# A hybrid encoder layer on one core: residual tiles of the down projection loaded further ahead into four buffers, and the hidden frames loaded by ScalarE's queue

## The chip, the cores and the metric

The kernel runs on one NeuronCore of a Trainium2 chip. TensorE multiplies; VectorE, ScalarE and GpSimd compute beside it; SyncE, ScalarE and GpSimd can each call DMA transfers, which all run on the core's 16 DMA engines. The metric is the device time of one execution in microseconds; lower is better. Each engine works through its own instructions in order and waits for the others by semaphores, so an instruction that waits holds up everything behind it on its engine.

## The reference

One layer of a streaming encoder over 576 frames (512 of a prompt, 64 of a sample), in float32. Attention and short convolution come first; the part that the change touches is the end, the feed-forward network with its residual:

```python
x = x + mix @ w_out
h2 = rmsnorm(x, g_norm2)
x = x + (jax.nn.silu(h2 @ w_gate) * (h2 @ w_up)) @ w_down
```

The model width is 2048, the hidden width D_FF 5632. The outputs are x and the new rows of the key, value and convolution caches.

## The kernel before

Everything is kept transposed: channels on the 128 partitions, the 576 frames as columns in two halves of 288. Every float32 operand is split into a high and a low part, and each product is made of three matmuls (high x high, low x high, high x low). The split of a weight takes ScalarE a cast and VectorE a subtraction; its result is the tile `whl` (L217, L218).

Gate, up and down projection run in *units*. A unit multiplies 256 output channels by 2m input blocks of 128 with a seven-product scheme in Strassen's manner: the weights are read as four quarters a11, a12, a21, a22, the frames come in seven prepared forms, and the products are numbered 1 to 7. Units 0 to 41 (NGU = 42) are gate and up, in turn; 42 to 77 are the 36 down units that the list `DOWN` names as (output pair d, first hidden pair, last hidden pair). There are 8 output pairs and 22 hidden pairs, so each output pair is worked on in several units; unit 42 takes (0, 0, 3), unit 47 (0, 3, 7), unit 53 (3, 4, 8), unit 70 is the first that finishes an output pair. Below, (41,4) is product 4 of unit 41. The products of neighbouring units are interleaved: (n+1,1), (n,3), (n,4), (n+1,2), (n+1,6), (n+1,7), (n+1,5). Their weights are prepared two products ahead in program order (`AHEAD`).

Four kinds of transfer run in the down units:

- **Weights**: two loads `raw` a unit on SyncE's queue (L180), rows of 512 B. There are two buffers for each, so a load waits until the unit two before it has used its own. VectorE's sum `s` (L1052) needs the second.
- **Frames**: the seven forms of a hidden pair. The up units write them, form by form (`form`, L923, GpSimd), to `hid_dram`. `load_pair` (L1141, GpSimd) reads one pair back into one of seven slots: 2016 KB, one row of 16,128 B for each partition. Three slots lie where the second norm's result was, four where its sums were; later pairs reuse a slot when all output pairs are past it. `calls` says after which unit.
- **Residual tiles**: `load_x2` (L1126, GpSimd) reads two blocks of 128 x 576 of x (576 KB) when the unit begins, into one of two buffers; the unit's seven products are added there (L1135, VectorE); after product 4 `store_x2` (L1130, GpSimd) writes it back for the next unit of the same output pair. A unit that finishes a pair turns its tile on TensorE and writes the output instead (`store_y`).
- **Outputs**, from unit 70 on, GpSimd and ScalarE.

Only TensorE's order is written out by hand. That of the other engines, SyncE's and GpSimd's DMA calls among them, is laid out by a scheduler from its own estimates when the kernel is built: an instruction that can go earlier by them stands earlier in its engine's order, whatever its place in the program.

Of the kernel before, what the change touches and what calls it, by code (L numbers as in the profile page):

```python
# [10 lines left out]
F32 = mybir.dt.float32  # L11
# [5 lines left out]
P = 128  # L17
TP = 512
TS = 64
T = TP + TS  # L20
HALF = T // 2
HALVES = ((0, HALF), (HALF, T))
# [15 lines left out]
SLOTS = 7  # L38
# [55 lines left out]
def tile_hybrid_stream_step(  # L94
# [6 lines left out]
    nc = tc.nc  # L101
# [14 lines left out]
    tmp = ctx.enter_context(tc.tile_pool(name="tmp", bufs=2, side="left"))  # L116
    acon = tc.alloc_tile_pool(name="acon", bufs=1, side="left")
    xt_dram = tc.dram_tile([KD, P, T], F32, name="xt_dram")
    x2_dram = tc.dram_tile([KD, P, T], F32, name="x2_dram")
    hid_dram = tc.dram_tile([NFP, P, FORMS, 2, HALF], F32, name="hid_dram")  # L120
# [23 lines left out]
    UNITS = [(kind, fp, 0, NP) for fp in range(1, NFP) for kind in ("gate", "up")]  # L144
    NGU = len(UNITS)
# [31 lines left out]
    def load_weight(i=None):  # L177
        i = len(raws) if i is None else i
        raws[i], raw3, src = weight_raw(i)
        nc.sync.dma_start(out=raw3, in_=src)  # L180
# [73 lines left out]
    def misc(name):  # L254
        return ps_z.tile([P, 512], F32, tag="misc", name=name, bufs=2)
# [104 lines left out]
    with tc.manual_schedule(engines={mybir.EngineType.Activation, mybir.EngineType.DVE, mybir.EngineType.SP}):  # L360
# [26 lines left out]
        for kt in range(KD + LAG):  # L387
# [19 lines left out]
            if kt in (14, 16):  # L407
                a = (kt - 14) * 512
# [53 lines left out]
    for i in range(5):  # L462
        n = P if i < 4 else TS
# [369 lines left out]
    h2pool = tc.alloc_tile_pool(name="h2pool", bufs=1, reuse_waits="tile", side="left")  # L833
# [168 lines left out]
    slots = {}  # L1002
# [13 lines left out]
    NU = len(UNITS)  # L1016
# [25 lines left out]
    def prepare(n, p_):  # L1042

        st = unit.setdefault(n, {})
        m = UNITS[n][3]
        if p_ == 1:
            st["a11"], st["a12"] = column(first_block + 2 * n, m)
        src = {1: "a11", 2: "a12", 3: "a12", 4: "a22", 5: "s1", 6: "a11", 7: "a21"}[p_]
        if p_ == 6:
            st["a21"], st["a22"] = column(first_block + 2 * n + 1, m)  # L1050
            st["s1"] = w2pool.tile([P, NP, P], F32, tag="s1", name="s1")[:, :m]
            nc.vector.tensor_tensor(out=st["s1"], in0=st["a21"], in1=st["a22"], op=ALU.add)  # L1052
            nc.vector.tensor_tensor(out=st["a21"], in0=st["a21"], in1=st["a11"], op=ALU.subtract)
            nc.vector.tensor_tensor(out=st["a11"], in0=st["s1"], in1=st["a11"], op=ALU.subtract)
        if p_ == 3:
            nc.vector.tensor_tensor(out=st["a12"], in0=st["a12"], in1=st["a11"], op=ALU.subtract)
        slot_turn[0] += 1
        whl = wpool.tile([P, 2, NP, P], F32R, tag=("whi", "wlo")[slot_turn[0] % 2], name="whl")[:, :, :m]
        split(whl[:, 0], whl[:, 1], st[src])
        operand[n, p_] = whl  # L1060
# [9 lines left out]
    def run(n, p_):  # L1070
        st = unit[n]
        kind, fp = UNITS[n][:2]

        def kept(tag):
            t = tmp.tile([P, HALF], F32, tag=tag, name="part", bufs=1)
            nc.scalar.copy(out=t, in_=st["y"])  # L1076
            return t

        def done(c, i, ps, part=None):
            if kind != "down":  # L1080
                return finish(kind, fp, c, i, ps, part)
            add(n, c, i, ps)
            if part is not None:
                add(n, c, i, part)
            if n in last:
                store_y(n, c, i)
            elif (c, i) == (1, 0):
                store_x2(n)

        if p_ == 1:  # L1090
            st["y"] = ps_pj.tile([P, HALF], F32, tag="pj", name="psy")
            multiply(st["y"], n, 1, True)
            st["p1"] = kept("ms")
        elif p_ == 2:
            x = ps_z.tile([P, 512], F32, tag="z0", name="psx2")[:, :HALF]
            multiply(x, n, 2, True)
            done(0, 0, x, st["p1"])
        elif p_ == 6:
            multiply(st["y"], n, 6, False)
            st["u2"] = kept("ms" if n == NGU - 1 else "t")  # L1100
        elif p_ == 7:
            st["w"] = ps_z.tile([P, 512], F32, tag=f"z{n % 2 + 1}", name="psw")[:, :HALF]
            multiply(st["w"], n, 7, True)
        elif p_ == 5:
            multiply(st["y"], n, 5, False)
            u4 = kept("acc")
            done(1, 1, st["w"], u4)
        elif p_ == 3:
            multiply(st["y"], n, 3, False)
            done(0, 1, st["y"])  # L1110
        else:
            multiply(st["w"], n, 4, False)
            done(1, 0, st["w"], st["u2"])
            del unit[n]


    last = {}
    for n in range(NGU, NU):
        last = {m_: 1 for m_ in last if UNITS[m_][1] != UNITS[n][1]} | {n: 1}
    xt2 = {}  # L1120
    down = {}

    def load_x2(n):
        d = UNITS[n][1]
        xt2[n] = down["pool"].tile([P, 2, T], F32, tag="x2", name=f"x2_{n}", bufs=2)
        nc.gpsimd.dma_start(out=xt2[n], in_=x2_dram[2 * d : 2 * d + 2].rearrange("k p t -> p k t"))  # L1126

    def store_x2(n):
        d = UNITS[n][1]
        nc.gpsimd.dma_start(out=x2_dram[2 * d : 2 * d + 2].rearrange("k p t -> p k t"), in_=xt2.pop(n))  # L1130

    def add(n, c, i, src):
        a, b = HALVES[i]
        dst = xt2[n][:, c, a:b]
        nc.vector.tensor_tensor(out=dst, in0=src, in1=dst, op=ALU.add)  # L1135

    def load_pair(p):
        tag = ("h2ah", "h2al", "b22", "s3", "s4", "s5", "s6")[p % SLOTS]
        pool = h2pool if p % SLOTS < 3 else down["pool"]
        slots[p] = pool.tile([P, FORMS, 2, HALF], F32R, tag=tag, name=f"slot{p}")  # L1140
        nc.gpsimd.dma_start(out=slots[p].bitcast(F32), in_=hid_dram[p])  # L1141

    def store_y(n, c, i):

        x2t, cs = xt2[n][:, c, :], slice((2 * UNITS[n][1] + c) * P, (2 * UNITS[n][1] + c + 1) * P)
        whole = (c, 1 - i) in unit[n].setdefault("done", set())
        unit[n]["done"].add((c, i))
        b0, b1 = ((0, 2), (3, 4), (0, 3), (2, 4))[2 * whole + i]

        def work():  # L1150
            yield 3
            ob = down["pool"].tile([P, 3, P], F32, tag="ob", name="ob", bufs=2)[:, : b1 - b0]
            po = misc("pot")[:, : (b1 - b0) * P]
            for q in range(b0, b1):
                nc.tensor.transpose(po[:, (q - b0) * P : (q - b0 + 1) * P], x2t[:, q * P : (q + 1) * P], ident)
            nc.vector.tensor_copy(out=ob, in_=po.rearrange("p (i c) -> p i c", c=P))
            nc.gpsimd.dma_start(out=yp[b0 * P : b1 * P, cs].rearrange("(i p) c -> p i c", p=P), in_=ob)
            if i:
                po2 = misc("pot2")
                nc.tensor.transpose(po2[:TS, :P], x2t[:, TP:], ident)  # L1160
                os_ = down["pool"].tile([TS, P], F32, tag="obs", name="obs", bufs=2)
                nc.scalar.copy(out=os_, in_=po2[:TS, :P])
                nc.scalar.dma_start(out=ys[:, cs], in_=os_)

        pipe.spawn(work())
# [4 lines left out]
    for k_, (n, p_) in enumerate(order):  # L1170
        if p_ == 1:
            for i in range(first_block + 2 * n, min(first_block + 2 * n + 4, len(specs))):
                if i not in raws:
                    load_weight(i)
        if (n, p_) == (NGU, 1):
            tpool.release()
            ypool.release()
            down["pool"] = tc.alloc_tile_pool(name="dpool", bufs=1, reuse_waits="tile", side="right")
            load_x2(n)
            load_pair(3)  # L1180
        if n > NGU and p_ == 1:
            load_x2(n)
            if n < NGU + SLOTS - 3:
                load_pair(n - NGU + 3)
        if k_ + AHEAD < len(order):
            prepare(*order[k_ + AHEAD])
        run(n, p_)
        if n == NGU - 1:
            for p in {2: (0, 1), 3: (2,)}.get(p_, ()):
                load_pair(p)  # L1190
        if n >= NGU and p_ == 4:
            for p in calls[n - NGU]:
                load_pair(p)
    pipe.flush()
# [34 lines left out]
```

## Time and profile before

| | before |
|---|---|
| median of 3 runs | 2506.39 us (2503.45 to 2511.66) |
| the profiled execution's own time | 2504.79 us |
| its span, first to last instruction | 2503.1 us |
| TensorE busy | 2425.3 us (97%), mean granted clock 0.989 |
| VectorE, ScalarE, GpSimd busy | 70%, 43%, 11% |
| DMA | 369.52 MB, mean 148 GB/s |
| first frame called, last frame called | 1905.1 us, 2333.3 us |
| frames, call to landing | 22 loads, 10.5 us median (8.8 to 20.4) |
| residual tiles, call to landing | 36 loads, 4.6 us median (4.0 to 16.6) |

In the profile's rows PE is TensorE, DVE VectorE, ACT ScalarE, POOL GpSimd, SPq SyncE's sequencer; L1066 is a line of the kernel. `psy<-slot,whl` is a matmul that writes the tile psy from the tiles slot and whl. What stands in brackets after a row of the timeline is the idle time of its engine just before it, and what ended it. A row of the waits reads: who waited, for whom, total us, times, longest. The windows give, for each stretch of the span, the busy time of every engine, the granted TensorE clock as a share, the busy share of the DMA engines and what they moved. DMA queue q0 is GpSimd's, q1 SyncE's.

### The profile page before, as it was taken

The numbers are of one execution on the slowest core, as the hardware profiler recorded it, in microseconds if no ns is written. First come the engines' busy times: TensorE is split into PE (matmuls) and PEld (weight loads), VectorE is DVE, ScalarE is ACT, GpSimd is POOL, SyncE is SP. The second block draws the span as 40 slices with busy tenths as digits, with TensorE's granted clock in tenths as the row PEclk, the third lists the DMA queues.
The fourth block names the chain that finished last, engine by engine and source line by source line (L and its number), as shares of the span: only waits on it lengthen the run. The fifth ranks groups of instructions, "written<-read, shape, count | busy, mean of one in ns | idle before, by whom it ended". The sixth has DMA issues, their size and how long they took to land.

```text
span 2503.1 us, 43901 instructions
## 1 busy us (share of the span) xinstructions
PE 2425.3 (97%) x18121; PEld 2412.5 (96%) x18121; DVE 1756.5 (70%) x2772; ACT 1070.0 (43%) x1863; POOL 282.8 (11%) x483
## 2 busy tenths in 40 slices
PE   8999999999999999999999999999998897999898
PEld 8999999999999999999999999999998897999798
DVE  7766666353345458888888888888886686877676
ACT  6655555231122345444444444444443343444333
POOL 2111011110020120000010000100001111101121
PEclk9999999999999999999999999999999998999899
DMA  8322332222242333445344454444545767868753
GB/s 266 86 87 86 90 90 83 68 85 85 85 161 85 103 136 107 135 144 158 120 144 140 148 155 126 140 137 149 154 133 209 278 195 265 262 220 288 257 155 92
DMA packets 441345, 369.52 MB, mean 148 GB/s; under 512 B 9854, under 2 KB 411896, under 8 KB 438328
## 3 DMA queue, kind: packets, MB, share of 16 engines
q1 hardware_dynamic: 413624, 233.39, 32.2%
q0 software_dynamic: 26240, 132.79, 14.4%
q8 instruction: 142, 2.33, 0.4%
q10 hardware_dynamic: 1280, 0.53, 0.1%
q14 instruction: 59, 0.48, 0.1%
HBM read 285.85 MB, written 80.82 MB: 146 GB/s over the span
## 4 chain that ended last, share of the span: by engine, by line
PE 88%; DMA 5%; issue 3%; DVE 2%; ACT 1%; POOL 0%; SPq 0%; POOLq 0%; DVEq 0%; ACTq 0%
PE psy L1066 29%; PE pj L209 23%; PE psw L1066 15%; PE pjo L209 8%; PE psx L1066 7%; DMA raw<-in_w_down_dram 4%; PE pw L981 2%; DVE whl L218 1%; PE z L547 1%; PE po L613 1%; DMA xin<-in_x_prompt_dram 0%; DVE x L1135 0%; DMA slot<-hid_dram 0%; PE os L643 0%; PE zs L573 0%
## 5 line engine op out<-in xcount | busy, mean ns | idle before, releaser
L217 ACT CAST whl<-raw 128x1024 fp32r<-128x1024 f32 (+5 forms) x468 | 419.0, 897 | 309.0 <-issue 106.4
L218 DVE TENSOR_TENSOR whl<-raw,whl 128x1024 fp32r<-128x1024 f32 (+5 forms) x468 | 481.4, 1029 | 89.1 <-ACT whl L217 87.7
L209 PE MATMUL pj<-xhi,whi 128*128 128x288 f32 x1504 | 450.0, 299 | 0.4 <-ACT whi L172 0.4
L209 PE MATMUL pj<-xlo,whi 128*128 128x288 f32 x1504 | 444.3, 295 | 1.7 <-DVE xlo L343 1.7
L209 PE MATMUL pj<-xhi,wlo 128*128 128x288 f32 x1504 | 443.9, 295 | 0.3 <-DVE wlo L173 0.3
L1066 PE MATMUL psy<-slot,whl 128*128 128x288 f32 x2112 | 304.8, 300 | 47.0 <-ACT part L1076 20.3
L1066 PEld LDWEIGHTS psy<-slot,whl 128*128 128x128 f32 x2112 | 291.2, 192 | 49.9 <-ACT part L1076 21.3
L209 PEld LDWEIGHTS pj<-xlo,whi 128*128 128x128 f32 x1504 | 283.6, 189 | 2.0 <-DVE xlo L343 2.0
L1066 PE MATMUL psw<-tsum,whl 128*128 128x288 f32 x2016 | 282.6, 296 | 2.8 <-DVE ut L960 2.8
L209 PEld LDWEIGHTS pj<-xhi,whi 128*128 128x128 f32 x1504 | 283.8, 189 | 1.0 <-ACT whi L172 0.6
L209 PEld LDWEIGHTS pj<-xhi,wlo 128*128 128x128 f32 x1504 | 283.9, 189 | 0.9 <-DVE wlo L173 0.5
L1066 PE MATMUL psy<-tsum,whl 128*128 128x288 f32 x2016 | 281.1, 295 | 1.2 <-DVE whl L218 1.2
L1066 PEld LDWEIGHTS psw<-tsum,whl 128*128 128x128 f32 x2016 | 273.4, 190 | 3.0 <-DVE ut L960 3.0
L1066 PEld LDWEIGHTS psy<-tsum,whl 128*128 128x128 f32 x2016 | 271.8, 189 | 1.5 <-DVE whl L218 1.5
L172 ACT CAST whi<-raw 128x1024 fp32r<-128x1024 f32 (+1 forms) x138 | 140.0, 1031 | 231.7 <-PE pj L209 95.8
L1076 ACT COPY part<-psy 128x288 f32<-128x288 f32 x234 | 93.4, 399 | 296.9 <-PE psy L1066 290.7
L923 POOL DMA_DIRECT2D hid_dram<-form x154 | 83.6, 543 | 914.0 <-DVE form L218 751.2
L173 DVE TENSOR_TENSOR wlo<-raw,whi 128x1024 fp32r<-128x1024 f32 (+1 forms) x132 | 160.3, 1227 | 23.9 <-ACT whi L172 22.6
L1066 PE MATMUL psw<-slot,whl 128*128 128x288 f32 x1056 | 155.5, 298 | 2.2 <-DVE x L1135 2.2
L1066 PEld LDWEIGHTS psw<-slot,whl 128*128 128x128 f32 x1056 | 146.0, 190 | 2.5 <-DVE x L1135 2.4
L1066 PE MATMUL psy<-b,whl 128*128 128x288 f32 x1008 | 140.4, 295 | 0.5 <-ACT part L1076 0.5
L1066 PE MATMUL psx<-h2ah,whl 128*128 128x288 f32 x672 | 135.6, 297 | 2.7 <-DVE gs L960 2.7
(336 smaller groups left out, 4208.1 us busy)
## 6 DMA issues: line engine op xcount, KB each, us to landing
raw<-in_w_in_dram SPq DMA_DIRECT2D x47, 1024.0 KB, 5.6
raw<-in_w_gate_dram SPq DMA_DIRECT2D x44, 1024.0 KB, 5.7
raw<-in_w_up_dram SPq DMA_DIRECT2D x44, 1024.0 KB, 6.3
hid_dram<-form POOLq DMA_DIRECT2D x154, 288.0 KB, 2.5
slot<-hid_dram POOLq DMA_DIRECT2D x22, 2016.0 KB, 10.5
x<-x_dram POOLq DMA_DIRECT2D x36, 576.0 KB, 4.6
raw<-in_w_down_dram SPq DMA_DIRECT2D x30, 640.0 KB, 5.8
raw<-in_w_out_dram SPq DMA_DIRECT2D x16, 1024.0 KB, 5.2
```

The source lines that it names most:

```text
L172: nc.scalar.copy(out=hi[:, a:b], in_=raw[:, a:b])
L173: lo_eng.tensor_tensor(out=lo[:, a:b], in0=raw[:, a:b], in1=hi[:, a:b].bitcast(F32), op=ALU.subtract)
L209: mm(ps, w_[:, k, csl], x_[:, k, a:b], start=(k == 0 and n == 0), stop=(k == nk - 1 and n == 2))
L217: nc.scalar.copy(out=hi, in_=src)
L218: (lo_eng or nc.vector).tensor_tensor(out=lo, in0=src, in1=hi.bitcast(F32), op=ALU.subtract)
L547: mm(zb[i], a_[:, kk], b_[:, q0:TP], start=(n == 0), stop=False, skip_group_check=True)
L613: mm(po[:, i * P : 512], a_[:, i, :], b_[:, : 512 - i * P], stop=(i == 0 and n == 2), **kw)
L923: nc.gpsimd.dma_start(out=hid_dram[fp][:, n - 1], in_=t.bitcast(F32))
L981: mm(pss[j, i], w_[:, k, j * P : (j + 1) * P], x_, start=(kk == 0 and k == 0 and n == 0), stop=(kk == 1 and k == 7 and n == 2))
L1066: mm(ps, whl[:, w_, j, :], x_, start=(start and j == 0 and q == 0), stop=(j == len(xs_) - 1 and q == 2), skip_group_check=True)
L1076: nc.scalar.copy(out=t, in_=st["y"])
```

## The change

A residual tile is called in earlier, and there are four places for it instead of two. Units whose number leaves 0 or 1 by four, and all from unit 70 on, use the two whole buffers as before. The other 14 (42, 43, 46, 47, ... 66, 67) use four pieces of 128 x 288 each, in temporary tiles that the gate and up units leave (tags y, r, sq, hx); these are loaded and stored by four DMAs each. The call for unit n+2 stands after product 4 of unit n in the program; before it stood at product 1 of the unit itself. And `load_pair` calls its transfer on ScalarE instead of GpSimd.

```diff
+    first_last = min(last)
+    spare = [(tmp, "y"), (tmp, "r")], [(tmp, "sq"), (h2pool, "hx")]
+
     def load_x2(n):
-        d = UNITS[n][1]
-        xt2[n] = down["pool"].tile([P, 2, T], F32, tag="x2", name=f"x2_{n}", bufs=2)
-        nc.gpsimd.dma_start(out=xt2[n], in_=x2_dram[2 * d : 2 * d + 2].rearrange("k p t -> p k t"))
+
+        d, xb = UNITS[n][1], {}
+        if n % 4 < 2 or n >= first_last:
+            whole = down["pool"].tile([P, 2, T], F32, tag="x2", name=f"x2_{n}", bufs=2)
+            nc.gpsimd.dma_start(out=whole, in_=x2_dram[2 * d : 2 * d + 2].rearrange("k p t -> p k t"))
+            xb["whole"] = whole
+        for c in range(2):
+            for i, (a, b) in enumerate(HALVES):
+                if "whole" in xb:
+                    xb[c, i] = whole[:, c, a:b]
+                    continue
+                pool, tag = spare[n % 2][c]
+                xb[c, i] = pool.tile([P, HALF], F32, tag=tag, name=f"x2_{n}", bufs=2)
+                nc.gpsimd.dma_start(out=xb[c, i], in_=x2_dram[2 * d + c][:, a:b])
+        xt2[n] = xb
 
     def store_x2(n):
-        d = UNITS[n][1]
-        nc.gpsimd.dma_start(out=x2_dram[2 * d : 2 * d + 2].rearrange("k p t -> p k t"), in_=xt2.pop(n))
+        d, xb = UNITS[n][1], xt2.pop(n)
+        if "whole" in xb:
+            nc.gpsimd.dma_start(out=x2_dram[2 * d : 2 * d + 2].rearrange("k p t -> p k t"), in_=xb["whole"])
+            return
+        for c, i in ((0, 0), (1, 1), (0, 1), (1, 0)):
+            a, b = HALVES[i]
+            nc.gpsimd.dma_start(out=x2_dram[2 * d + c][:, a:b], in_=xb[c, i])
 
     def add(n, c, i, src):
-        a, b = HALVES[i]
-        dst = xt2[n][:, c, a:b]
+        dst = xt2[n][c, i]
...
     def load_pair(p):
...
-        nc.gpsimd.dma_start(out=slots[p].bitcast(F32), in_=hid_dram[p])
+        nc.scalar.dma_start(out=slots[p].bitcast(F32), in_=hid_dram[p])
...
             load_x2(n)
             load_pair(3)
-        if n > NGU and p_ == 1:
-            load_x2(n)
-            if n < NGU + SLOTS - 3:
-                load_pair(n - NGU + 3)
+            load_x2(n + 1)
+        if NGU < n < NGU + SLOTS - 3 and p_ == 1:
+            load_pair(n - NGU + 3)
...
         if n >= NGU and p_ == 4:
+            if n + 2 < NU:
+                load_x2(n + 2)
             for p in calls[n - NGU]:
                 load_pair(p)
```

In the order that the scheduler gives the changed kernel, the call for a tile on GpSimd stands right after the store that frees its place, some two units earlier than before: that of unit 52 after the store of unit 48. The pieces of units 42 and 43 and the whole tiles of 44 and 45 stand among the last stores of `form`. On ScalarE the calls for slots 0 to 3 stand between the casts of the last forms, and the cast for (42,6) stands behind two of these casts, where it stood ahead of them before. On VectorE the weight part of (41,4) now stands ahead of the sum `s` of unit 42, where it stood behind it. TensorE's order is unchanged.

More of the change, by code (lines that the diff above doesn't have):

```diff
@@ L1140, in load_pair @@
         slots[p] = pool.tile([P, FORMS, 2, HALF], F32R, tag=tag, name=f"slot{p}")
-        nc.gpsimd.dma_start(out=slots[p].bitcast(F32), in_=hid_dram[p])
+        nc.scalar.dma_start(out=slots[p].bitcast(F32), in_=hid_dram[p])
     def store_y(n, c, i):
-        x2t, cs = xt2[n][:, c, :], slice((2 * UNITS[n][1] + c) * P, (2 * UNITS[n][1] + c + 1) * P)
+        x2t, cs = xt2[n]["whole"][:, c, :], slice((2 * UNITS[n][1] + c) * P, (2 * UNITS[n][1] + c + 1) * P)
         whole = (c, 1 - i) in unit[n].setdefault("done", set())
```

## Prediction

> **What bounds the kernel now.** TensorE carries the chain, so I read the last stage, the only one that the change touches, by windows, and then TensorE's waits in it.
>
> ```profile
> PE 88%; DMA 5%; issue 3%; DVE 2%; ACT 1%; POOL 0%; SPq 0%; POOLq 0%; DVEq 0%; ACTq 0%
> ```
> ```profile
> core 0: us, PE busy (x) PEld busy (x) DVE busy (x) ACT busy (x) POOL busy (x), PEclk, DMA share, GB/s
> 1905.00:1990.00 85.00, 64.36 (x435) 63.11 (x433) 47.58 (x92) 27.19 (x55) 12.78 (x21) 0.90 0.82 301
> ...
> 2060.00:2100.00 40.00, 22.63 (x157) 21.94 (x156) 18.83 (x37) 9.98 (x20) 5.09 (x8) 0.83 0.86 319
> 2100.00:2310.00 210.00, 210.00 (x1564) 209.81 (x1564) 167.27 (x258) 87.53 (x144) 25.23 (x37) 0.99 0.78 250
> 2310.00:2365.00 55.00, 41.70 (x296) 40.66 (x295) 36.44 (x61) 17.75 (x32) 6.52 (x10) 0.88 0.70 256
> ```
> ```profile
> PE psy L1066 <- ACT part L1076: 20.3, 4, 13.8
> PE psy L1066 <- DVE whl L218: 17.9, 4, 9.3
> PE psy L1066 <- DMA slot<-hid_dram: 8.8, 2, 7.3
> ```
>
> From 2100 to 2310 TensorE is busy all the time. It loses 20.6 us in 1905:1990 (window A), 17.4 in 2060:2100 (B) and 13.3 in 2310:2365 (C), and the granted clock is down in exactly these. The waits name ScalarE and VectorE, but behind each the chain of waits has a weight load:
>
> ```profile
> 1943.93 20.48 DMA raw<-in_w_down_dram
> ...
> 2066.09 23.94 DMA raw<-in_w_down_dram
> ...
> 2326.29 21.60 DMA raw<-in_w_down_dram
> ```
>
> Why some take over 20 us, the DMA view of 2072:2082 shows:
>
> ```profile
> DMA packets 571, 4.24 MB, mean 424 GB/s; under 512 B 32, under 2 KB 317, under 8 KB 317
> ...
> q0 software_dynamic: 285, 4.08, 95.6%
> q1 hardware_dynamic: 285, 0.15, 4.8%
> ```
>
> The engines are full, and the two queues send packet for packet, 285 each. GpSimd's queue (q0) carries frames there, whose packet is one partition's row (7 x 2 x 288 x 4 = 16,128 B); SyncE's (q1) carries weights in rows of 512 B. So beside frames the weights get 15 GB/s: **a weight load called during a burst of frames lands when the burst has drained.** By the Trainium skill (DMA: Bandwidth & Descriptors, Queues, rings and completion order) an engine drains a packet of some 9 to 17 descriptors before it turns to the next queue; the trace has single rows in turn, and I go by the trace.
>
> **The residual tiles (x2).** Their cost in waiting is small:
>
> ```profile
> DVE x L1135 <- DMA x<-x_dram: 2.0, 1, 2.0
> ```
> ```profile
> 2091.10 6.49 PE L1066 MATMUL psy<-slot,whl 128*128 128x288 f32 x36 [13.76 <-ACT part L1076]
> 2099.76 2.14 PE L1066 MATMUL psw<-slot,whl 128*128 128x288 f32 x12 [2.16 <-DVE x L1135]
> ```
>
> VectorE waits once for such a load, TensorE 2.16 us behind it. With four buffers a load waits for the store of four units ago instead of two; the tile of unit 53 is then in place before window B. Gain 2.2 us; none if the prefetch isn't early enough. The price: 14 of the 36 units (42, 43, 46, 47, ... 67) move their tile as four pieces, 8 DMAs for 2, so 84 more on GpSimd, at up to 0.73 us (rows below) 61 us. GpSimd is busy 12 to 15% of these windows and computes nothing; I take 0. If that cover were gone, a late piece costs like the 2.16 us above. Bytes stay the same.
>
> **The frames on ScalarE's queue.** The calls on GpSimd in B and C before:
>
> ```profile
> 2060.47 0.57 POOL L1141 DMA_DIRECT2D slot<-hid_dram  x1 [6.35 <-PE psw L1066]
> 2064.08 0.71 POOL L1130 DMA_DIRECT2D x_dram<-x  x1 [3.04 <-DVE x L1135]
> 2064.79 1.65 POOL L1141 DMA_DIRECT2D slot<-hid_dram  x3
> ...
> 2313.01 0.72 POOL L1126 DMA_DIRECT2D x<-x_dram  x1 [3.03 <-DMA x_dram<-x]
> 2317.20 0.55 POOL L1141 DMA_DIRECT2D slot<-hid_dram  x1 [3.46 <-PE psw L1066]
> 2320.84 0.71 POOL L1130 DMA_DIRECT2D x_dram<-x  x1 [3.09 <-DVE x L1135]
> 2321.68 0.57 POOL L1141 DMA_DIRECT2D slot<-hid_dram  x1
> ...
> 2332.56 0.73 POOL L1130 DMA_DIRECT2D x_dram<-x  x1 [3.10 <-DVE x L1135]
> 2333.29 0.55 POOL L1141 DMA_DIRECT2D slot<-hid_dram  x1
> ```
>
> Frames stand behind a store that waits for the unit's last add: three by some 3 us in B, one by some 3.5 and one by 2 in C. On ScalarE they go as soon as TensorE frees the slot.
>
> What ScalarE pays is the issue: 0.37 us is the median of a weight load on SyncE, 0.55 that of a frame on GpSimd.
>
> ```profile
> L180 SPq DMA_DIRECT2D raw<-in_w_down_dram x68: 367/368/5317, 1943.0 to 2455.0; - x68
> ```
> ```profile
> 2062.19 0.52 ACT L217 CAST whl<-s 128x384 fp32r<-128x384 f32 x1 [1.86 <-PE psw L1066]
> ```
>
> 22 issues at 0.5 are 11 us on an engine that is busy 25 to 42% here. Behind each stand the cast for the product three ahead and a copy of a partial sum. In B the four issues (2.0 us, from 2060.5) fit ScalarE's own gap of 1.86 us before 2062.19. So 0 in the steady part; the upper bound of an issue is the 5.3 us of SyncE's longest (a rival below).
>
> *B.* Before the weights called at 2066 landed at 2090, there moved four frames of 2.06 MB, a tile's load and two stores (1.77 MB) and the weights (1.05 MB), 11.1 MB. The change moves as much, units 50 and 51's pieces out and 54 and 55's in. But the frames are all called by 2062, so the engines are full from about 2061.3, and 26.2 us at 424 GB/s later, at 2087.5, all is through: 2.5 us earlier. Sum for B: -2.5 - 2.2 = **-4.7** (bounds -7 and 0).
>
> *C.* Of the two frames from 2317 the second comes 4.5 us earlier, and the load of unit 68's tile, at 2313 before, is long done. Both frames have then drained by about 2329 (4.13 + 0.7 MB at 424 = 11.4 us from 2318), and the weight loads called at 2324.6 and 2326.3 (1.84 MB) go from there. The last frame comes at 2331 instead of 2333.3 and interrupts them, to about 2338; the rest, some 1.1 MB, lands by 2343 instead of 2347.9. **-5** (bounds -8 and +1).
>
> *A* is the other way. Its rows:
>
> ```profile
> 1920.82 0.56 DVE L1052 TENSOR_TENSOR s<-raw 128x384 f32<-128x384 f32 x1 [10.13 <-DMA raw<-in_w_down_dram]
> ...
> 1923.53 0.76 PE L1066 MATMUL psw<-tsum,whl 128*128 128x288 f32 x2 [2.79 <-DVE ut L960]
> ```
> ```profile
> 1927.41 0.55 POOL L1141 DMA_DIRECT2D slot<-hid_dram  x1 [0.36 <-PE psw L1066]
> 1931.01 0.54 POOL L923 DMA_DIRECT2D hid_dram<-form  x1 [3.05 <-DVE ut L931]
> ```
> ```profile
> 1937.42 0.43 ACT L217 CAST form<-ut 128x288 fp32r<-128x288 f32 x1 [6.36 <-DMA hid_dram<-form]
> ```
> ```profile
> 1936.63 1.09 PE L1066 MATMUL psy<-slot,whl 128*128 128x288 f32 x3 [7.33 <-DMA slot<-hid_dram]
> ...
> 1939.68 1.83 PE L1066 MATMUL psy<-slot,whl 128*128 128x288 f32 x9
> ...
> 1966.52 3.01 PE L1066 MATMUL psy<-slot,whl 128*128 128x288 f32 x11 [6.82 <-DVE whl L218]
> ```
> ```profile
> 1964.44 0.69 DVE L1052 TENSOR_TENSOR s<-raw 128x512 f32<-128x512 f32 x1 [7.60 <-DMA raw<-in_w_down_dram]
> ```
> ```profile
> DMA packets 3544, 12.81 MB, mean 400 GB/s; under 512 B 233, under 2 KB 2227, under 8 KB 3047
> ```
> ```profile
> q0 software_dynamic: 26240, 132.79, 14.4%
> ```
>
> In the built order of the changed kernel VectorE does the weight parts of (41,4) ahead of the waiting sum s (L1052), so the 2.79 us shrink by 1.6 and the third frame is called 1.6 earlier, landing some 3 us earlier. But GpSimd now calls pieces of x2_42 and the whole x2_44 and x2_45 ahead of the last stores of hidden forms: 1.77 MB stand before the store that left at 1931.01, in a queue that shares with frames. Leaving frames out, q0's packets average 3.7 KB over the kernel (the page's 26,240 packets and 132.79 MB less 22 x 128 and 45.4), so beside frames it gets 3.7/19.8 = 19%, 80 GB/s. Two frames (4.13 MB) keep the engines until about 1938, some 1 MB of the 1.77 has gone by then, the rest takes 2 us at 400, and that store lands at about 1941.5, not 1937.4. ScalarE, in order, waits there with a form cast, and ahead of the cast of (42,6) now, which was done at 1930.55 before. (42,6), at 1939.68 before, starts at about 1943.5, and the next weight loads, unit 44's, are called 4 us later, into a burst that now holds slots 4 to 6 at once. By the DMA view of 1930:1962 (the row of 3,544 packets) 12.81 MB moved before those weights were in, with the edges 13.3; the change adds slot 6, x2_45 and a part of x2_46, 2.8 MB. 16.1 MB at 400 GB/s are 40 us, from 1926, and 1 us is idle while slot 4 stands behind ScalarE: the second weight load lands at 1967 instead of 1964.4, +2.6. VectorE's sum of these weights now stands ahead of the parts of (44,1), which was done during the wait before: 12 matmuls at 210.00/1564 = 0.134 us, +1.6. Slot 6 is no longer called in among the next weights; of the four waits for whl two are small (17.9 less 9.3 and 6.82 leaves 1.8 us), and I take one of them as gone: -1. **+3** (bounds -2, if frames and x2 share better than I think, and +9, if ScalarE's wait moves all that follows by its 4 us and more).
>
> Sum: +3 - 4.7 - 5 = -6.7 us, bounds -17 and +10, against 2504.8 for the profiled execution (span 2503.1 and 1.7 around it). The median before, 2506.4, lies 1.6 above that, so I forecast **2499.5**.
>
> **Rivals.** *Moved, not gained* (2507): the engines are full in all three windows and bytes don't change, so weights land when they did; A's +3 and the 2.2 remain. By the Trainium skill (the same page, Issuing engines are not separate DMA queues) queues only save issue time, which comes to this. For it: 424 GB/s in the burst. Against: frames held 3 us behind stores. Chance 0.25.
>
> *Weights get more* (2490): if the third queue cuts a frame's row into packets near x2's 3.7 KB, weights get 512/4.2K = 12%, 51 GB/s; over the 19 us from 2066 to the end of B's frames that is nearly all of their 1.05 MB, and they land 6 us earlier there, as much in C, and A's store, with half of the bandwidth, is no longer late (-2): -6 - 2.2 - 6 - 2 = -16. Against: q1 shows whole rows as packets, and the third queue carries no long row here. The Trainium skill (the same page, SWDGE vs HWDGE vs iDMA) calls 4,096 B preferable for a packet; the frames' 16,128 B on q0 don't keep to that. Chance 0.12.
>
> *ScalarE held at its issue* (2516, slower): SyncE's issue took up to 5.3 us when its queue was backed up. If frames are pushed so, ScalarE stands in B for 4 x 5.3 us from 2060.5 instead of 2; the products that TensorE does from 2064 until its 13.76 us wait begins at 2077.3 then come after the burst, +13, and +3 to +5 in A and C, against the -7: +9.5. It decides once the four pushes exceed about 4 us. Against: a frame has 128 rows, a weight load 1,024. The store wait in A beyond 1945 gives the same sign. Chance 0.18.
>
> **Chances.** Forecast 0.45, with its own range 2492 to 2505. About 0.3% (7.5 us) is what a measurement of this kernel tells from no change: the border lies at 2498.9, through the forecast. Half of it, the 0.12 and a little make 0.38 faster; the other half and *moved* 0.42 same; 0.20 slower. Range 2487 to 2516.
>
> **What would show it.** Right: window B's weight load lands by 2087 in place of 2090, no 2.16 us wait at unit 53, the 9.3 us wait in C halved; in A a form cast that waits until about 1941 and TensorE idle before (42,6). Wrong: frames' issues over 1 us on ScalarE; weights over 15 GB/s beside frames; idle time in 2100:2310; waits for pieces of x2.

## The result, and the profile after

| | before | after |
|---|---|---|
| median of 20 runs each | 2505.47 us | 2512.34 us |
| ratio after / before (95% interval) | | 1.0026 (1.0015 to 1.0037) |
| span of the profiled execution | 2503.1 us | 2508.2 us |

The change costs 0.26%, some 6.5 us; the forecast was a gain of 7. The runs before lie between 2496 and 2515 us, those after between 2510 and 2519, so a single trace carries some us of chance. To see where it went, the windows after (us, then TensorE's busy time, the other engines', granted clock, DMA share):

```profile
1905.00:1990.00 85.00, 59.77 (x397) 58.23 (x396) 46.69 (x90) 24.68 (x49) 18.36 (x33) 0.84 0.86 308
2060.00:2100.00 40.00, 28.21 (x193) 27.64 (x192) 20.83 (x41) 11.29 (x24) 7.61 (x14) 0.83 0.87 320
2100.00:2310.00 210.00, 201.18 (x1491) 199.78 (x1490) 157.16 (x244) 83.69 (x136) 37.69 (x64) 0.99 0.75 244
2310.00:2365.00 55.00, 45.61 (x323) 44.68 (x322) 37.75 (x66) 19.72 (x36) 5.96 (x10) 0.94 0.76 261
```

Window A lost 4.6 us of TensorE's time, B and C gained 5.6 and 3.9, and the stretch between them, which had no idle time before, lost 8.8. Windows stand still while the work shifts, so I also compared like with like: ScalarE copies a partial sum (`part<-psy`, L1076) 111 times from 1898.5 us on, in every kernel here. The difference in start between the same copy in two traces says how far one kernel is behind at that point. Between the copies that start at 1898.5, 2051.5, 2122.8, 2312.2, 2364.4 and 2490.5 us before (1898.6, 2056.2, 2121.0, 2321.9, 2370.8, 2495.7 after) the change lost

| | A | B | between | C | rest | sum |
|---|---|---|---|---|---|---|
| forecast | +3 | -4.7 | 0 | -5 | 0 | -6.7 |
| measured | +4.6 | -6.5 | **+11.5** | -3.3 | -1.1 | +5.2 |

One term is wrong by 11.5 us; the others are near. Its rows, TensorE's idle times between B and C:

```profile
2151.07 2.67 PE L1066 MATMUL psy<-slot,whl 128*128 128x288 f32 x18 [0.76 <-DMA slot<-hid_dram]
...
2163.02 5.20 PE L1066 MATMUL psy<-slot,whl 128*128 128x288 f32 x37 [1.15 <-DVE whl L218]
...
2206.43 2.27 PE L1066 MATMUL psy<-slot,whl 128*128 128x288 f32 x15 [1.15 <-DVE whl L218]
2212.16 6.45 PE L1066 MATMUL psy<-slot,whl 128*128 128x288 f32 x35 [3.46 <-DVE whl L218]
```

Two more of 1.15 us follow at 2266.29 and 2309.70, and one at 2333.52 in C. Each of the five of 1.15 us stands some 8 to 9 us behind a frame's call on ScalarE (slots 12, 14, 16, 18 and 20), and each moves all later copies by 1.42 us. VectorE shows what happens at 2163:

```profile
2158.26 0.46 DVE L1154 TENSOR_TENSOR x<-part,x 128x288 f32<-128x288 f32 x1
2161.77 0.46 DVE L1154 TENSOR_TENSOR x<-psw,x 128x288 f32<-128x288 f32 x1 [3.05 <-PE psw L1066]
2162.15 0.82 DVE L218 TENSOR_TENSOR whl<-s,whl 128x640 fp32r<-128x640 f32 x1
```

VectorE waits 3.05 us for the end of a product (`psw`, to be added to x), and only then makes the weight part that TensorE needs next, although ScalarE's cast for it was done at 2156.6. Before, the same part stood ahead of that add: it was made from 2157.64 to 2158.5, 4 us before its product.

```profile
2157.64 0.82 DVE L218 TENSOR_TENSOR whl<-s,whl 128x640 fp32r<-128x640 f32 x1
...
2163.03 0.45 DVE L1135 TENSOR_TENSOR x<-psw,x 128x288 f32<-128x288 f32 x1
```

So the call is not paid in time on ScalarE (0.33 us) but in the **order**: behind these calls VectorE's weight part stands behind an add that waits 3.05 us, at five places as changed (2161.77, 2205.19, 2265.05, 2308.46, 2332.27) and at none before. Behind the calls for slots 11, 13 and 17 an add waits 2.3 us in the same way; that stops TensorE nowhere at once, but the one of slot 13 makes a weight load late, as the next rows show. What in the scheduler's estimates moves them is not shown.

The 3.46 us at 2212 are a weight load that meets a frame, from the chain of waits and the DMA view of 2203:2207:

```profile
2193.88 16.04 DMA raw<-in_w_down_dram
```
```profile
DMA packets 225, 1.69 MB, mean 422 GB/s; under 512 B 4, under 2 KB 99, under 8 KB 133
...
q10 hardware_dynamic: 94, 1.48, 88.3%
q0 software_dynamic: 36, 0.16, 9.7%
q1 hardware_dynamic: 95, 0.05, 4.0%
```

Rows of 512 B and of 16,128 B in turn again (95 and 94), 12 GB/s for the weights. The frame of slot 14 sends its first row at 2201.1 before and 2201.3 after, the same; but the load was called at 2192.43 before and at 2193.88 after, since SyncE waits for VectorE to be done with the buffer, and VectorE, by its new order, made three weight parts in a row only from 2191.57, after 2.31 us of waiting for a product. Before, the last row was in at 2201.85; after, 0.33 MB were left when the frame began and 0.18 MB at 2202, and came in until 2209.4. (A load's landing is the end of its last row, counted through SyncE's queue in order.)

The stop of 3.46 us costs some 5.2, since TensorE's granted clock is down behind it. The first row is after; the second, before, is the stretch with the same products:

```profile
2212.20:2218.50 6.30, 6.30 (x36) 6.30 (x37) 4.84 (x6) 0.40 (x1) 1.08 (x2) 0.73 0.66 178
```
```profile
2204.60:2211.30 6.70, 6.70 (x52) 6.70 (x52) 6.67 (x10) 3.21 (x5) 0.72 (x1) 1.00 0.83 286
```

At 0.73 instead of 1.00, 6.3 us lose some 1.7, and 3.46 + 1.7 = 5.2. Behind a stop of 1.15 us alone the granted clock stayed at 1.00 (2163:2168.2).

### The profile page after: what moved, and what is told of

It is laid out like the page before. It is cut to its first block, busy times and chain, and to the rows that moved or that the text cites. A ratio compares the mean times of both kernels' runs of the same rounds, so it can differ in the third digit from the quotient of the medians.

```text
span 2508.2 us, 44014 instructions
## 1 busy us (share of the span) xinstructions
PE 2429.6 (97%) x18121; PEld 2415.6 (96%) x18121; DVE 1756.1 (70%) x2772; ACT 1069.1 (43%) x1863; POOL 311.5 (12%) x545
## 4 chain that ended last, share of the span: by engine, by line
PE 90%; DMA 4%; DVE 2%; issue 2%; ACT 1%; POOL 0%; SPq 0%; POOLq 0%; ACTq 0%; DVEq 0%
PE psy L1066 30%; PE pj L209 23%; PE psw L1066 15%; PE pjo L209 8%; PE psx L1066 7%; DMA raw<-in_w_down_dram 3%; PE pw L981 2%; DVE whl L218 1%; DMA hid_dram<-form 1%; PE z L547 1%; PE po L613 1%; DMA slot<-hid_dram 0%; PE os L643 0%; PE zs L573 0%; DVE x L1154 0%
## 5 line engine op out<-in xcount | busy, mean ns | idle before, releaser
L1066 PE MATMUL psy<-slot,whl 128*128 128x288 f32 x2112 | 310.5, 303 | 55.2 <-ACT part L1076 19.5
L1076 ACT COPY part<-psy 128x288 f32<-128x288 f32 x234 | 93.2, 398 | 327.5 <-PE psy L1066 325.6
## 6 DMA issues: line engine op xcount, KB each, us to landing
slot<-hid_dram ACTq DMA_DIRECT2D x22, 2016.0 KB, 11.8
```

The costliest lines, as they stand in the source:

```text
L1066: mm(ps, whl[:, w_, j, :], x_, start=(start and j == 0 and q == 0), stop=(j == len(xs_) - 1 and q == 2), skip_group_check=True)
```

## The experiments

Theory O, from these rows: the loss is the order behind ScalarE's calls, and a weight load that comes too late to pass ahead of a frame. Rival G: it is GpSimd, which now waits 176 us for stores of pieces. Later, theory Q: what matters most is whether weights are called ahead of frames *in one queue*. The stages are those of the table above, against the trace of before. PE is TensorE's busy time in 2130:2300, 170 us, by the windows. One trace stands for each kernel: pairs with the same frame calls differ by up to 2.5 us in A (-2.7 and -5.2, -6.7 and -8.1) and by 0.6 between B and C (11.5 and 12.1, 17.3 and 17.7), so a few us in A say little. The trace of before ran in 2504.8 us, while the medians of before beside the experiments were 2506.6 to 2509.6, so the stages read worse than the ratios by some us.

| kernel | ratio to before (95%) | A | B | between | C | PE |
|---|---|---|---|---|---|---|
| as changed | 1.0026 (1.0015 to 1.0037) | +4.6 | -6.5 | +11.5 | -3.3 | 162.33 |
| tiles alone, frames on GpSimd | 1.0014 (1.0001 to 1.0027) | -2.7 | -2.6 | +17.3 | -3.7 | 156.54 |
| frames alone on ScalarE | 1.0005 (0.9995 to 1.0015) | +2.8 | -4.2 | +9.9 | -1.9 | 162.97 |
| ScalarE in B and C only | 0.9991 (0.9976 to 1.0006) | -5.2 | -7.5 | +17.7 | -3.4 | 157.65 |
| changed, frames on SyncE | 0.988 (0.9867 to 0.9894) | -6.7 | -7.8 | -0.2 | -9.7 | 170.00 |
| before, frames on SyncE | 0.9918 (0.9899 to 0.9937) | -1.9 | -5.0 | -0.2 | -7.4 | 170.00 |
| slots 12, 14, 16, 18 on SyncE | 0.9966 (0.9953 to 0.9979) | +3.3 | -6.0 | +0.4 | -2.4 | 169.73 |
| slots 0 to 6 on SyncE | 0.9959 (0.9945 to 0.9974) | -8.3 | -7.1 | +12.1 | -1.9 | 161.47 |
| all on SyncE, three behind weights | 0.9853 (0.983 to 0.9876) | -8.1 | -13.8 | -1.8 | -8.1 | 170.00 |
| changed, frames in rows of 2,304 B | 1.0025 (1.0011 to 1.0039) | +5.8 | -2.9 | +6.9 | -2.0 | 165.75 |
| three behind weights, rows of 2,304 B | 0.986 (0.9835 to 0.9884) | -13.0 | -11.9 | -1.8 | -7.8 | 170.00 |

**The residual tiles alone**

```diff
-        nc.scalar.dma_start(out=slots[p].bitcast(F32), in_=hid_dram[p])
+        nc.gpsimd.dma_start(out=slots[p].bitcast(F32), in_=hid_dram[p])
```

> The changed kernel with the frames called on GpSimd again: the residual tiles' half of the change alone. Theory O (order and own queue): the new idle time of the steady part (8.8 us in 2100:2310 of the changed kernel) comes from the frames' calls on ScalarE, so TensorE is busy again all through 2100:2310; the five stalls of 1.15 us and the weight load of 15.5 us are gone; window B keeps only the 2.2 us of the wait for x that goes; A, with pieces ahead of the last form stores, 0 to +4. Sum -2 to +3 us, ratio 0.999 to 1.001. Rival G (GpSimd): the loss comes from the 84 more DMAs, for whose stores GpSimd waits 176 us in the changed kernel; the frames, in the same queue again, stand behind these waits, so this kernel is slower than the changed one: +6 us and more against before, ratio 1.003 or above, with idle time in 2100:2310.

The stalls behind `whl` shrink to 0.8 us in all in 2100:2310, as O says, but others take their place, as G says: TensorE waits for frames.

```profile
2154.54 4.69 PE L1066 MATMUL psy<-slot,whl 128*128 128x288 f32 x18 [6.62 <-DMA slot<-hid_dram]
2201.79 2.67 PE L1066 MATMUL psy<-slot,whl 128*128 128x288 f32 x18 [2.97 <-DMA slot<-hid_dram]
2219.95 4.18 PE L1066 MATMUL psy<-slot,whl 128*128 128x288 f32 x18 [3.09 <-DMA slot<-hid_dram]
```

GpSimd's rows show why: a piece's load waits for the store that frees its place, and the frame stands behind it.

```profile
2202.87 1.69 POOL L1140 DMA_DIRECT2D x<-x_dram  x3 [8.10 <-DMA x_dram<-x]
2204.63 0.56 POOL L1150 DMA_DIRECT2D x_dram<-x  x1
2210.99 0.54 POOL L1140 DMA_DIRECT2D x<-x_dram  x1 [5.80 <-DMA x_dram<-x]
2211.52 0.54 POOL L1160 DMA_DIRECT2D slot<-hid_dram  x1
```

Slot 14 is called at 2211.5 instead of 2197.5. So with the tiles called this early their loads hold up the frames in GpSimd's order. The ratio of 1.0014 lies between the theories: G's waits are there, and neither had the gain in A.

**The frames alone** (the kernel before, with `nc.scalar` for `nc.gpsimd` in `load_pair`)

> The kernel before with the frames called on ScalarE: the frames' half alone. Theory O: the whole loss of the steady part is here, some 11 us by the lag of ScalarE's copies (five stalls of 1.15 us idle and 1.4 us of delay each, one weight load of 15 us that meets a frame, 5 us); B gains 3 (the weights land earlier, the wait of 2.2 us for x stays), C 3; A 0 to +3, since the form stores have no pieces ahead of them. Sum +5 to +8 us, ratio 1.002 to 1.003. Rival G: no idle time in 2100:2310, B and C gain: -5 us, ratio 0.998.

O is right in place: 9.9 us between B and C, with the same stalls, without any piece of a tile. VectorE's 2,772 instructions stand, by operation and tile, in exactly the order that they have as changed, so the early tiles have no part in it.

```profile
2163.55 6.14 PE L1066 MATMUL psy<-slot,whl 128*128 128x288 f32 x44 [1.15 <-DVE whl L218]
2210.55 8.45 PE L1066 MATMUL psy<-slot,whl 128*128 128x288 f32 x50 [4.73 <-DVE whl L218]
2266.68 6.10 PE L1066 MATMUL psy<-slot,whl 128*128 128x288 f32 x44 [1.15 <-DVE whl L218]
2309.76 5.33 PE L1066 MATMUL psy<-slot,whl 128*128 128x288 f32 x38 [1.15 <-DVE whl L218]
```

The ratio of 1.0005 is below the 1.002 it gave, and can't be told from 1, while the profiled execution is 7.5 us longer than that of before, which was a short one: the trace places the loss, the runs make it smaller.

**ScalarE in windows B and C alone**

```diff
-        nc.scalar.dma_start(
+        (nc.scalar if p in (7, 8, 9, 10, 19, 20, 21) else nc.gpsimd).dma_start(
```

> The changed kernel with only the frames of slots 7 to 10 and 19 to 21 (windows B and C) called on ScalarE, the other 15 on GpSimd. Theory O: the five stalls go but for the one behind slots 19 to 21, and the weight load called ahead of slot 14 lands in time: 0 to +2 in the steady part, B -6, C -3, A 0 to +4 as in the kernel with the tiles alone: -3 to -8 us, ratio 0.997 to 0.999. Rival G: the steady part loses as in the changed kernel, ratio 1.001 to 1.004.

The ratio can't tell; the stages do. B gains what it gained, and the stretch between loses 17.7 us to late frames, as with the tiles alone. That O left out what GpSimd's queue costs was its miss.

**All frames on SyncE**

```diff
-        nc.scalar.dma_start(out=slots[p].bitcast(F32), in_=hid_dram[p])
+        nc.sync.dma_start(out=slots[p].bitcast(F32), in_=hid_dram[p])
```

> The changed kernel with the frames called on SyncE. ScalarE's and VectorE's orders have none of the changes behind the frames' calls. Theory O: the five stalls go (7 us). A frame then stands in one queue with the weights: a weight load called ahead of it is through before it, one called behind it waits for it whole (2.06 MB at 424 GB/s, 5 us, when nothing else runs), as it did beside it. In the steady part 0 to +3, in B the weights behind four frames land at about the same time as in the changed kernel; SyncE waits in order for the slot to be free, which can hold the next weights: 0 to +4. Sum -5 to +4, ratio 0.998 to 1.002. Rival (one queue is worse): SyncE held at a frame's call keeps weights from being called in A, B and C, +10 us and more, ratio 1.004 or above.

Far better than either theory: 1.2% faster than before. Between B and C nothing is lost, as O says. The rest is in A, B and C. SyncE's rows in A:

```profile
1950.10 1.82 SPq L180 DMA_DIRECT2D raw<-in_w_down_dram  x2
1952.22 0.62 SPq L1160 DMA_DIRECT2D slot<-hid_dram  x1
1960.39 1.73 SPq L180 DMA_DIRECT2D raw<-in_w_down_dram  x2
1962.41 0.76 SPq L1160 DMA_DIRECT2D slot<-hid_dram  x1
```

The weights of unit 44, called at 1950.1 ahead of the frame of slot 5, land at 1953.7 and 1957.0, after 3.6 and 5.5 us; as changed they were called at 1952.2 beside three frames, and took 14.2 and 16.6. In one queue what is called first is through first. This is theory Q. A rival stands beside it in A: SyncE also calls the frames of slots 2, 3 and 4 earlier, at 1921.08, 1921.86 and 1922.66, where ScalarE, held by form casts, called them at 1924.58, 1933.27 and 1943.81. So there an earlier call and the order in the queue come together, and no run parts them; in B the run with three frames behind the weights does.

**The frames on SyncE without the early tiles** (the kernel before, with `nc.sync`)

> The kernel before with the frames called on SyncE, the residual tiles as before. Theory Q (one queue in order): what counts is that weights called ahead of a frame are through before it, and frames called ahead of weights delay them only by themselves. Then most of the gain is here: A -5 (weights of unit 44 ahead of the frames of slots 5 and 6), B -4 (the wait of 2.2 us for x stays), C -9, steady 0: -15 to -22 us, ratio 0.991 to 0.994. Rival P (the prefetch is needed: with the tiles as before, their loads in two buffers and not the frames set the time once the frames are out of GpSimd's queue): 0 to -8 us, ratio 0.997 to 1.000, with waits for x in A and B.

Q's forecast holds (ratio 0.9918): most of the gain comes with the frames on SyncE, by their earlier calls or by the queue. With the early tiles the ratio was 0.988: A gains 6.7 us with them instead of 1.9, and TensorE's wait in B is 9.7 us instead of 13.2.

**Four frames on SyncE**

```diff
-        nc.scalar.dma_start(
+        (nc.sync if p in (12, 14, 16, 18) else nc.scalar).dma_start(
```

> The changed kernel with the frames of slots 12, 14, 16 and 18 called on SyncE, the others on ScalarE as changed. Theory O (order and own queue): of the five stalls of 1.15 us the four behind these frames go (each 1.42 us of delay, 5.7 in all), and the second weight load of unit 61, which took 15.5 us, is through ahead of slot 14's frame in its own queue and takes 8 to 9 (5 us). A, B and C stay as changed: -10 us against the changed kernel, -3 to -6 against before, ratio 0.9975 to 0.999. Rival (the stalls belong to any frame on ScalarE, and move to slots 11, 13, 15 and 17): only the 5 us go, ratio 1.000 to 1.002.

The stretch between loses 0.4 instead of 11.5 us, and the load of 15.5 us takes 10.0; the kernel is now 0.34% faster than before, a little more than expected. The rival falls: slots 11, 13, 15 and 17 are still called on ScalarE, and no stall of TensorE follows them, though the adds behind 11, 13 and 17 still wait 2.3 us. As changed, too, a stall followed only the second of two calls within 15 us of each other.

**The frames of window A on SyncE**

```diff
-        nc.scalar.dma_start(
+        (nc.sync if p < 7 else nc.scalar).dma_start(
```

> The changed kernel with the frames of slots 0 to 6, those of window A, called on SyncE, the others on ScalarE as changed. Theory Q: the weights of unit 44 land some 12 us earlier, as in the kernel with all frames on SyncE (1957 instead of 1969), and ScalarE's form casts have no frame ahead of them; A goes from +4 to -6 or -7, the rest stays: steady +12, B -6, C -3. Sum -3 to -7 against before, ratio 0.997 to 0.999. Rival (A is late because of the pieces of the residual tiles ahead of the last form stores, not because of the frames' queue): A stays at 0 to +4 and the ratio at 1.001 to 1.003.

A goes from +4.6 to -8.3 us with the pieces of the tiles still among the last form stores, and the other stages stay within 1.5 us. So the frames' calls on ScalarE made A slow, not the pieces; the frames of slots 2 to 4 were called by 1924.2 here. The ratio, 0.9959, is a little below the forecast. TensorE's waits in A, as changed and then with this edit:

```profile
1944.81 2.59 PE L1066 MATMUL psy<-slot,whl 128*128 128x288 f32 x9 [8.11 <-ACT part L1076]
1968.91 0.61 PE L1066 MATMUL psy<-slot,whl 128*128 128x288 f32 x1 [6.96 <-ACT whl L217]
1971.30 3.90 PE L1066 MATMUL psy<-slot,whl 128*128 128x288 f32 x16 [1.78 <-DVE whl L218]
```
```profile
1938.66 2.53 PE L1066 MATMUL psy<-slot,whl 128*128 128x288 f32 x9 [2.94 <-ACT part L1076]
1948.24 6.06 PE L1066 MATMUL psy<-slot,whl 128*128 128x288 f32 x30 [5.41 <-ACT part L1076]
```

The wait for weights is gone, and that before (42,6) shrinks from 8.11 to 2.94 us.

**Three frames behind the weights in B**

```diff
+            if n == NGU + 10:
+                for p in (8, 9, 10):
+                    load_pair(p)
...
             for p in calls[n - NGU]:
-                load_pair(p)
+                if n != NGU + 8 or p == 7:
+                    load_pair(p)
```

> The changed kernel with all frames on SyncE, and the frames of slots 8, 9 and 10 called behind the weights of unit 53 instead of ahead of them. Theory Q: in B these weights were called at 2059.8 behind four frames and landed at 2078.7 and 2080.9, and TensorE waited 9.7 us. Behind one frame only they land by 2068, and the frames, needed by units 54 and later, land at about 2084: -6 to -10 us against the kernel with all frames on SyncE, ratio to before 0.984 to 0.986. Rival (moved, not gained: unit 54 then waits for the frames of slots 8 and 9 as long as unit 53 waited for its weights): within 2 us of the kernel with all frames on SyncE, ratio 0.987 to 0.989.

With all frames on SyncE the weights of unit 53 now stand ahead of three of the four frames. They land at 2061.8 and 2064.2, after 3.5 and 5.0 us instead of 18.9 and 20.2, and B's idle time falls from 10.0 us to 3.8:

```profile
2062.21 1.87 PE L1066 MATMUL psy<-slot,whl 128*128 128x288 f32 x12 [0.33 <-DMA slot<-hid_dram]
2081.35 5.97 PE L1066 MATMUL psy<-slot,whl 128*128 128x288 f32 x24 [9.68 <-ACT whl L217]
```
```profile
2084.66 0.61 PE L1066 MATMUL psy<-slot,whl 128*128 128x288 f32 x1 [3.57 <-ACT whl L217]
2085.52 6.17 PE L1066 MATMUL psy<-slot,whl 128*128 128x288 f32 x26 [0.25 <-DVE whl L218]
```

The first fence is the kernel with all frames on SyncE, the second this one. At 0.9853 (median 2475.22 us; the quotient of the medians is 0.987) it is the fastest kernel so far. Its interval overlaps that of all frames on SyncE, but its slowest of 4 runs (2478.1) is below the fastest of 4 there (2479.3). What is late now are the next unit's weights, called behind these frames: they take 13.9 and 14.7 us.

**Smaller rows**

```diff
-    hid_dram = tc.dram_tile([NFP, P, FORMS, 2, HALF], F32, name="hid_dram")
+    hid_dram = tc.dram_tile([NFP, FORMS, P, 2, HALF], F32, name="hid_dram")
...
-        nc.scalar.dma_start(out=slots[p].bitcast(F32), in_=hid_dram[p])
+        nc.scalar.dma_start(
+            out=slots[p].bitcast(F32).rearrange("p f h t -> p f (h t)"), in_=hid_dram[p].rearrange("f p h t -> p f (h t)")
+        )
```

> The changed kernel, frames on ScalarE's queue, every engine's order as changed; only the layout of the hidden forms in memory differs, so that a frame is read in rows of 2,304 B (seven for each partition) instead of one of 16,128 B. Theory R (queues take turns row by row): beside a frame the weights get 512/2,816 = 18% of some 420 GB/s, 76 GB/s, instead of 10 to 16. The second weight load of unit 61 lands some 5 us earlier (15.5 us to 10), the weights in B (1.05 MB, called at 2073) after 14 us instead of 19, 5 us earlier, those in C and A 5 and 3 to 5 earlier; the five stalls of 1.15 us stay. -12 to -20 us against the changed kernel, ratio to before 0.995 to 0.998. Rival S (the share goes by queue or by bytes, not by rows): weights starve as before, ratio 1.000 to 1.004.

Theory R's mechanism is right, its time is not. Rows still go in turn, 971 of frames and 973 of weights in 2084:2092, so the weights get 0.49 MB in 8 us, 62 GB/s, five times as much:

```profile
DMA packets 2089, 3.15 MB, mean 394 GB/s; under 512 B 79, under 2 KB 1037, under 8 KB 2088
...
q10 hardware_dynamic: 971, 2.20, 70.8%
q1 hardware_dynamic: 973, 0.49, 20.7%
```

The load of 15.5 us takes 10.9, and the stretch between gains 4.6 us with every order as changed: that is most of the 5.2 us that were the collision, and the stalls of 1.15 us (still there) are the larger part of the rest. The ratio alone would fit rival S; the rows decide for R. But the longest frame takes 16.0 instead of 13.1 us (the median is the same, 11.7 and 11.8), in B the second weight load still takes 17.5 us (19.0 as changed), and there ScalarE shows a new cost:

```profile
2066.20 10.11 ACTq L1160 DMA_DIRECT2D slot<-hid_dram  x4
2076.40 0.51 ACT L217 CAST whl<-s 128x384 fp32r<-128x384 f32 x1 [10.08 <-issue]
```

Four calls of 896 rows each hold it for 10 us, where four of 128 rows took 2.05; TensorE stands for 5.55 us behind it.

The same rows in the fastest kernel:

> The fastest kernel so far (all frames on SyncE, the frames of slots 8 to 10 behind the weights of unit 53) with rows of 2,304 B for the frames. Theory R: weights and frames are in one queue in order, so the weights gain nothing; what GpSimd's queue moves beside frames (residual tiles, forms) loses some of its share, since it no longer takes turns with rows of 16,128 B: wrong way round, it gains, as its own rows are 1,152 to 2,304 B and a turn of the other queue is shorter. The frame after it then lands later by as much. -2 to +2 us, ratio 0.984 to 0.987. Rival S: no change at all in any landing, the same ratio.

0.986 (0.9835 to 0.9884): no difference that can be measured.

## Why the prediction was wrong, point by point

**The step that failed** is the zero for the steady part ("22 issues at 0.5 are 11 us on an engine that is busy 25 to 42% here ... So 0 in the steady part"). The duration was on the safe side:

```profile
L1160 ACTq DMA_DIRECT2D slot<-hid_dram x22: 326/326/716, 1904.8 to 2339.7; - x22
```

I asked what the call costs ScalarE, and named the cast and the copy behind it, but not what it does to the scheduler's order of VectorE: weight parts moved behind adds that wait for TensorE. That order can be read from the built program before any run, and "idle time in 2100:2310" stood among the signs of being wrong. The zero became 11.5 us: 5.7 for four stalls of 1.42, 5.2 for the load at 2193.88, 1.0 for a wait for slot 11's frame, less 0.4 that came back. Calling four frames on SyncE took it to 0.4.

**Window A**, +3 forecast, +4.6 measured: many parts came as said (the third frame landed 3.5 us earlier, 3 was said; the form cast waited until 1941.8, 1941.5 was said; TensorE was idle before (42,6), which started at 1944.8, not 1943.5). The weights were called 8.8 us later, not 4, and their last row landed 5.5 us later (1969.3), not 2.6. But the cause was half wrong, and that the number is near is in part luck. The sum put the late cast on the tiles' pieces ahead of the form stores; the cast of (42,6), as changed, then with the frames alone, then with the tiles alone:

```profile
1943.96 0.51 ACT L217 CAST whl<-raw 128x384 fp32r<-128x384 f32 x1
```
```profile
1943.98 0.51 ACT L217 CAST whl<-raw 128x384 fp32r<-128x384 f32 x1
```
```profile
1931.72 0.51 ACT L217 CAST whl<-raw 128x384 fp32r<-128x384 f32 x1
```

Without any piece it is as late as changed; with the pieces and without the calls it is some 12 us earlier. What held it is its place behind the form casts, which the prediction had too and which comes with the frames' calls.

**Window B**, -4.7 forecast, -6.5 measured. With all work 4.7 us late the weights landed 1.7 us later than before, a gain of 3.0 (2.5 was said), and the wait of 2.16 us for x went. The four calls took 2.05 us, 2.0 was said.

**Window C**, -5 forecast, -3.3 measured: the wait of 9.33 us became two of 2.77 and 4.06, and a stall behind slots 19 and 20, the same order again, takes 1.42 of the gain.

**The rivals.** *Weights get more* falls: the third queue sent whole rows, 12 GB/s were left for weights. *Moved, not gained* falls in B and C: measured against the work around them the weights did land earlier, by 3.0 us in B. *ScalarE held at its issue* did not occur (0.72 us at most), and the reason given against it, a frame's 128 rows against a weight load's 1,024, fits the runs in part: with 896 rows a call took up to 5.93 us. But on SyncE a frame's call of 128 rows took 4.55 us behind two weight loads of 1,792 rows each (slot 21), so the rows already in the queue count too. The slower side that came true was none of the three: it was an order.

**By the Trainium skill** (DMA: Bandwidth & Descriptors, Queues, rings and completion order) a packet of some 9 to 17 descriptors drains before the engine turns. After as before the trace has single rows in turn (95 and 94, and 12 and 12 in the quarter of a us from 2204.25; 971 and 973), so the trace decides. The Trainium skill (the same page, Issuing engines are not separate DMA queues) says that calling on several engines saves issue time and no more. Here moving the frames to SyncE was worth 0.8% with the tiles as before and 1.5% with the early tiles (0.988 against 1.0026), through the time of the call, the order in a queue and the orders of the engines.

## What to carry to other kernels

A DMA call that was moved to another engine cost less here in its issue (0.33 us) than in what it did to orders (some 11 us): read the built order of that engine, and of those that feed the same consumer, around every call. Where it can be arranged, put large transfers into the queue of the small, urgent ones, behind them, and not into a queue of their own beside them: here the urgent load that was called first in one queue was through first (3.5 and 5.0 us in B, against 18.9 and 20.2 called behind four frames), and beside a queue with rows of 16,128 B it got one small row for each large one.

## What was not expected of the hardware

- A frame's call on ScalarE took 0.33 us (0.72 at most) with 128 rows of 16,128 B; with 896 rows of 2,304 B, the same 2 MB, it took 0.37 us in the median and 5.93 where four followed one another. On SyncE one with 128 rows took 4.55 us behind two weight loads.
- With frames in rows of 2,304 B all queues together moved 396 GB/s in 2077:2085, with the long rows 416 in the same stretch: 5% less.
- Behind stops of TensorE of 1.15 and 3.46 us close together the granted clock was 0.73 for 6.3 us; behind one of 1.15 us alone it stayed at 1.00.
